# Six input projections of a fused transformer kernel started on x times its gain, ahead of the RMS norm

## The chip, the cores and the metric

The kernel runs on one core of a Trainium2 chip. TensorE (PE) multiplies, VectorE (DVE) and ScalarE (ACT) work on elements, GpSimd (POOL) does a few of them too, and SyncE (SP) issues the DMA transfers. Each engine takes the instructions of its own queue in order and waits on semaphores for the others. The metric is the time of the program on the device in microseconds, lower is better; the median of several runs counts.

## The reference, cut to what matters

Two transformer blocks over 512 tokens of width 1024 follow one another in fp32. The change touches the first steps only: the RMS norm of x with its gain, and the product with `w_in`.

```python
def rms_norm(x, g):
    y = xf * lax.rsqrt(jnp.mean(xf * xf, axis=-1, keepdims=True) + RMS_EPS)
    return y * g

h = rms_norm(x, norm_mix)
p = h @ w_in
p_rw = p_rw + (token_shift(p_rw) - p_rw) * mu_shift
r, k, v, wd, ad, gd, cb, cc, cx, ga, gb = jnp.split(p, offsets, axis=-1)
out_a = rwkv7_branch(r, k, v, wd, ad, gd, ...)
```

The branch makes a decay and a gate out of `wd` and `ad` by small (LoRA) products, a second gate out of `gd`, and a recurrence over the tokens out of r, k and v. Since 1/rms is one number per token, (x * gain / rms) @ w_in is the same as ((x * gain) @ w_in) / rms.

## The kernel before

Everything lies with the features on the 128 partitions and the 512 tokens along the free axis: x is 8 columns of 128x512, `w_in` is cut into blocks of 128 output features. Fp32 products go through three matmuls: each operand is split into a rounded high part (a cast, by ACT) and a low part (a subtraction, by DVE), and `mm_fm` adds high by high (line 182), high by low (183) and low by high (184) into one PSUM bank of 128x512. A block is 8 steps of three matmuls, 24 in all. `wload` brings half a block of weights per transfer (`wraw`, five buffers) and `wsplit` splits it into `whi` (four buffers) and `wlo` (three); the first two blocks, loaded with `early=True`, are split with POOL in place of DVE, into `we`.

The start runs like this. Four transfers bring x in pairs of columns. For each column ACT squares it (203, 206) and DVE and POOL in turn add the squares (207, 208). `sums` forms the sum over the partitions with small matmuls (146), `rsqrt` makes 1/rms by three Newton steps on DVE (134 to 139, tiles `rq_v`, `rq_t`, `rq_y`), `bcast` spreads it over all partitions by matmuls with the identity (192). Then, for each of the 8 columns, DVE forms `hx` = x * gain / rms (212), reading 1/rms from PSUM, and `split` makes `h` from it (152 and 153). Only then can a block of `w_in` be multiplied.

Blocks are used in this order: block 0 (`sa`: wd and ad), 1 and 2 (`sg`, `gsp`: gd), then, in four rounds of `prep`, k, r and v: blocks 3, 4, 5 in round 0, blocks 6, 7, 8 in round 1 and so on. `shift` mixes a block with its neighbour token: ACT scales it into `q` (236), DVE adds (237). `sa` goes through a tanh and a split to `wa`, which the LoRA products of each round need (`lora_mm`, 274). In a round the norm of k is a small product (292, from the square `sq`), eleven short DVE steps, `rb`, and a broadcast (314); a scan `cs` over the tokens gives the decay; then come `kk`, `f`, `m`, three pieces of `KB`, `r`, `rkk` and `vs`, with POOL doing some products (`f`, two of `AR`) among them. `prep_tail` (340, 344) of a round, the small products of `rkk` and `vs`, is called in the next round behind that round's k.

The code is ordered by the framework's scheduler, which puts each engine's instructions into a fixed queue before the run; pools with few buffers add waits on the readers of the older tile. The three pools of PSUM banks are `mm` (three banks), `sc` (two) and `ch` (three; they are first used in the chunks of the recurrence, far later).

Of the kernel before, what the change touches and what calls it, by code (L numbers as in the profile page):

```python
# [26 lines left out]
PI_BELOW = 3.1415925  # L27

# [17 lines left out]
def fused_kernel(ctx, tc, a, out):  # L46
# [72 lines left out]
    for i in range(4):  # L119
        nc.sync.dma_start(x0[:, 2 * i:2 * i + 2], a["xT"][:, 2 * i:2 * i + 2])  # L120
        if i == 0:
            nc.sync.dma_start(vc, a["vecs"])
# [35 lines left out]
    def wsplit(raw, shape, early=False):  # L158
        if early:
            w = reg.tile([128, 2] + shape[1:], F32R, tag="G4", bufs=4, name=nm("we"))  # L160
            split(raw, w[:, 0], w[:, 1], eng=G)
            return w[:, 0], w[:, 1]
# [78 lines left out]
    shift(proj_in(0, True), 12, sa)  # L241
# [955 lines left out]
```

## Time and profile before

| | us |
|---|---|
| median of 3 runs | 1345.91 |
| lowest, highest | 1342.25, 1346.05 |
| profiled execution, its own time | 1346.67 |
| its span in the profile | 1344.7 |

| engine | busy us | share of the span |
|---|---|---|
| PE (matmul) | 1303.4 | 97% |
| PE (weight load) | 1073.8 | 80% |
| DVE | 821.7 | 61% |
| ACT | 524.0 | 39% |
| POOL | 176.1 | 13% |

The times in the rows below are microseconds from the start of the span. A row of the timeline is one or several like instructions in a row: start, time they took together, engine, line, operation, output and inputs, and in brackets the idle time before it with what ended it. Neighbouring instructions of DVE and ACT overlap by some 0.05 us, so a pass shown with 0.69 us comes 0.62 us behind another. Matmuls overlap too: what counts is the distance of their starts.

### The profile page before, as it was taken

The numbers are of one execution on the slowest core, as the hardware profiler recorded it, in microseconds if no ns is written. First come the engines' busy times: TensorE is split into PE (matmuls) and PEld (weight loads), VectorE is DVE, ScalarE is ACT, GpSimd is POOL, SyncE is SP. The second block draws the span as 40 slices with busy tenths as digits, with TensorE's granted clock in tenths as the row PEclk, the third lists the DMA queues.
The fourth block names the chain that finished last, engine by engine and source line by source line (L and its number), as shares of the span: only waits on it lengthen the run. The fifth ranks groups of instructions, "written<-read, shape, count | busy, mean of one in ns | idle before, by whom it ended". The sixth has DMA issues, their size and how long they took to land.

```text
span 1344.7 us, 18356 instructions
## 1 busy us (share of the span) xinstructions
PE 1303.4 (97%) x6640; PEld 1073.8 (80%) x6640; DVE 821.7 (61%) x1640; ACT 524.0 (39%) x948; POOL 176.1 (13%) x185
## 2 busy tenths in 40 slices
PE   3999999999999999999999999999999999999997
PEld 2777888888879888878888888888878777788886
DVE  5677574848466755656844636544777566663455
ACT  4444332322335444454423423324344465333332
POOL 5113002010120020002021020120322000100003
PEclk9999998989999999999999999999999999999999
DMA  4222341323315522153644635323234223233331
GB/s 143 87 84 68 102 116 44 92 67 108 101 50 150 194 94 86 56 159 111 192 134 126 191 98 164 110 87 96 95 124 133 71 63 118 94 95 101 95 118 63
DMA packets 85211, 143.95 MB, mean 107 GB/s; under 512 B 21473, under 2 KB 21601, under 8 KB 85121
## 3 DMA queue, kind: packets, MB, share of 16 engines
q1 hardware_dynamic: 85120, 142.78, 34.2%
q8 instruction: 52, 0.85, 0.3%
q14 instruction: 39, 0.31, 0.1%
HBM read 136.19 MB, written 5.24 MB: 105 GB/s over the span
## 4 chain that ended last, share of the span: by engine, by line
PE 94%; DVE 3%; POOL 1%; DMA 1%; issue 0%; ACT 0%; SPq 0%; DVEq 0%; ACTq 0%; POOLq 0%
PE mm L182 26%; PE mm L183 25%; PE mm L184 25%; PE mm L628 1%; PE mm L627 1%; PE mm L629 1%; PE ch L986 1%; PE sc L386 1%; PE ch L948 1%; PE ch L467 1%; PE ch L458 1%; DMA x<-in_xT 1%; PE ch L462 1%; PE ch L491 1%; PE ch L443 0%
## 5 line engine op out<-in xcount | busy, mean ns | idle before, releaser
L152 ACT CAST whi<-wraw 128x512 fp32r<-128x512 f32 x406 | 251.6, 622 | 540.5 <-PE mm L183 468.8
L153 DVE TENSOR_TENSOR wlo<-wraw,whi 128x512 fp32r<-128x512 f32 x406 | 299.4, 739 | 222.3 <-PE mm L184 116.0
L182 PE MATMUL mm<-h,whi 128*128 128x512 f32 x328 | 131.6, 401 | 1.0 <-DVE k L237 1.0
L183 PE MATMUL mm<-h,whi 128*128 128x512 f32 x328 | 130.6, 398 | 0.0
L184 PE MATMUL mm<-h,wlo 128*128 128x512 f32 x328 | 130.1, 397 | 0.0
L182 PE MATMUL mm<-x2g,whi 128*128 128x512 f32 x256 | 100.2, 392 | 0.0
L184 PE MATMUL mm<-x2g,wlo 128*128 128x512 f32 x256 | 99.7, 390 | 0.0
L183 PE MATMUL mm<-x2g,whi 128*128 128x512 f32 x256 | 99.6, 389 | 0.0
L182 PE MATMUL mm<-ff,whi 128*128 128x512 f32 x256 | 99.6, 389 | 0.0
L183 PE MATMUL mm<-ff,whi 128*128 128x512 f32 x256 | 99.6, 389 | 0.0
L184 PE MATMUL mm<-ff,wlo 128*128 128x512 f32 x256 | 99.6, 389 | 0.0
L182 PEld LDWEIGHTS mm<-h,whi 128*128 128x128 f32 x328 | 62.3, 190 | 16.0 <-DVE k L237 2.6
L184 PEld LDWEIGHTS mm<-h,wlo 128*128 128x128 f32 x328 | 62.0, 189 | 13.1 <-issue 0.5
L183 PEld LDWEIGHTS mm<-h,whi 128*128 128x128 f32 x328 | 62.1, 189 | 12.7 <-issue 0.4
L852 POOL TENSOR_TENSOR X<-X,d 128x512 f32<-128x512 f32 x24 | 39.3, 1636 | 220.8 <-DVE d L850 220.8
L658 POOL TENSOR_TENSOR gt<-gt,nsq 128x512 f32<-128x512 f32 x21 | 27.7, 1321 | 291.4 <-ACT nsq L657 284.0
L182 PE MATMUL mm<-h2a,whi 128*128 128x512 f32 x152 | 60.7, 402 | 0.1
L183 PE MATMUL mm<-h2a,whi 128*128 128x512 f32 x152 | 60.3, 397 | 0.0
L184 PE MATMUL mm<-h2a,wlo 128*128 128x512 f32 x152 | 60.2, 396 | 0.0
L182 PE MATMUL mm<-h2b,whi 128*128 128x512 f32 x152 | 60.0, 394 | 0.0
L184 PE MATMUL mm<-h2b,wlo 128*128 128x512 f32 x152 | 59.5, 393 | 0.0
L183 PE MATMUL mm<-h2b,whi 128*128 128x512 f32 x152 | 59.4, 392 | 0.0
(467 smaller groups left out, 2724.1 us busy)
## 6 DMA issues: line engine op xcount, KB each, us to landing
wraw<-in_w_in SPq DMA_DIRECT2D x162, 256.0 KB, 2.6
wraw<-in_w_up SPq DMA_DIRECT2D x64, 256.0 KB, 2.6
wraw<-in_w_down SPq DMA_DIRECT2D x64, 256.0 KB, 2.8
adaraw<-in_w_ada SPq DMA_DIRECT2D x24, 512.0 KB, 3.7
wraw<-in_w_proj_b SPq DMA_DIRECT2D x16, 256.0 KB, 2.7
wraw<-in_w_k SPq DMA_DIRECT2D x16, 256.0 KB, 2.7
wraw<-in_w_proj_a SPq DMA_DIRECT2D x16, 256.0 KB, 2.7
wraw<-in_w_v SPq DMA_DIRECT2D x16, 256.0 KB, 2.7
```

The lines of the kernel that those rows point to most:

```text
L152: S.copy(hi, src)
L153: eng.tensor_tensor(lo, src, hi.bitcast(F32), op=ALU.subtract)
L182: PE.matmul(acc, lhsT=wh, rhs=xh, start=start and k == 0, stop=False)
L183: PE.matmul(acc, lhsT=wh, rhs=xl, start=False, stop=False)
L184: PE.matmul(acc, lhsT=wl, rhs=xh, start=False, stop=stop and k == n - 1)
L386: PE.matmul(pq[hd % 2][:, j * 128:(j + 1) * 128], lhsT=KB[p0:p0 + 64, j, n * 128:(n + 1) * 128], rhs=AR[p0:p0 + 64, j, n].rearrange("p q c ...
L458: PE.matmul(pu[ub:ub + 32, hs], lhsT=ZT[ub:ub + 32, c, hd, :], rhs=gsb[ub:ub + 32, hs], start=True, stop=True)
L462: PE.matmul(pg[ub + 32:ub + 64, hd * 64:(hd + 1) * 64], lhsT=gr[ub:ub + 32, hd, 32:64], rhs=VU[ub:ub + 32, tb, c, hd, :], start=False, sto ...
L467: PE.matmul(pu[ub + 32:ub + 64, hs], lhsT=ZT[ub + 32:ub + 64, c, hd, :], rhs=gsb[ub + 32:ub + 64, hs], start=True, stop=True)
L491: PE.matmul(py[kb:kb + 64, hd * 64:(hd + 1) * 64], lhsT=gr[:, hd, 64:128], rhs=VU[:, tb, c, hd, :], start=n == 0 and hd == 0, stop=hd == 7)
L658: G.tensor_tensor(self.acc, self.acc, sq, op=ALU.add)
L852: G.tensor_tensor(X[:, j], X[:, j], d, op=ALU.add)
```

## The change

Six transfers bring x now, one or two columns each, and between them go the first halves of the weights of blocks 0 to 5 (`first_weights`), with their second halves behind. As each column of x lands, `split` forms the high and low part of x * gain (`xg`, no 1/rms in it). The twelve halves of weights are split by ACT and DVE into `wf` and `we`. `first_mm(j)` multiplies column j with all six blocks; their six sums stand in six PSUM banks, three of `mm` and three of `ch`. The squares are added by DVE alone. The sums over the partitions are put behind the matmuls of column 5, the broadcast of 1/rms behind those of column 6. ACT copies 1/rms from PSUM to `rxs`; six DVE passes scale the six banks by it into `pf` (line 251 of the new code), and `proj_in` hands these out for blocks 0 to 5. `h` is formed behind that as before, from `rxs`, for the blocks from 6 on. The split with POOL is gone.

```diff
+    nc.sync.dma_start(x0[:, 0], a["xT"][:, 0])
+    nc.sync.dma_start(vc, a["vecs"])
+    first_weights(0, 0)
+    first_weights(1, 0)
+    nc.sync.dma_start(x0[:, 1], a["xT"][:, 1])
+    for i, j in ((2, 2), (3, 3), (4, 4), (5, 6)):
+        first_weights(i, 0)
+        nc.sync.dma_start(x0[:, j:min(j + 2, DB) if j > 3 else j + 1],
+                          a["xT"][:, j:min(j + 2, DB) if j > 3 else j + 1])
+    for i in range(NFIRST):
+        first_weights(i, 1)
...
+    first = [mmbank() for _ in range(3)] + [chbank() for _ in range(3)]
...
+    def first_mm(j):
+        for blk in range(NFIRST):
+            w = wf_[blk, j // 4]
+            cs_ = slice((j % 4) * 128, (j % 4 + 1) * 128)
+            mm_fm(first[blk], [(w[:, 0, cs_], w[:, 1, cs_])], [xg[j]], start=j == 0, stop=j == DB - 1)
+
     for j in range(DB):
-        acc = accx[j % 2]
-        if j < 2:
-            S.activation(acc, x0[:, j], AF.Square)
+        split(x0[:, j], xg[j][0], xg[j][1], scale=vcol("norm_mix", j))
+        if j % 4 == 0:
+            first_split(j // 4)
+        if j == 0:
+            S.activation(accx, x0[:, j], AF.Square)
         else:
             sq = tt("sqx")
             S.activation(sq, x0[:, j], AF.Square)
-            (V, G)[j % 2].tensor_tensor(acc, acc, sq, op=ALU.add)
-    V.tensor_tensor(accx[0], accx[0], accx[1], op=ALU.add)
-    rxb = bcast(rsqrt(sums(accx[0]), TB, 1.0 / D, 1e-6))
+            V.tensor_tensor(accx, accx, sq, op=ALU.add)
+        if j < DB - 2:
+            first_mm(j)
+    ssx = sums(accx)
+    first_mm(DB - 2)
+    rxb = bcast(rsqrt(ssx, TB, 1.0 / D, 1e-6))
+    first_mm(DB - 1)
+    rxs = tt("rxs")
+    S.copy(rxs, rxb)
+    pf = []
+    for blk in range(NFIRST):
+        f = tt("pf")
+        V.tensor_tensor(f, first[blk], rxs, op=ALU.mult)
+        pf.append(f)
...
     for j in range(DB):
         hf = tt("hx")
-        V.scalar_tensor_tensor(hf, x0[:, j], vcol("norm_mix", j), rxb, op0=ALU.mult, op1=ALU.mult)
+        V.scalar_tensor_tensor(hf, x0[:, j], vcol("norm_mix", j), rxs, op0=ALU.mult, op1=ALU.mult)
         split(hf, h[j][0], h[j][1])
...
-    def proj_in(blk, early=False):
+    def proj_in(blk):
+        if blk < NFIRST:
+            return pf[blk]
         p = mmbank()
-        mm_fm(p, wload(a["w_in"][blk], 0, DB, early), h)
+        mm_fm(p, wload(a["w_in"][blk], 0, DB), h)
         return p
...
-    shift(proj_in(0, True), 12, sa)
+    shift(proj_in(0), 12, sa)
```

How the queues change is seen from the instructions in their order. On DVE before, from the last step of 1/rms to the tile `k` of block 3 (names: output, then inputs; `wlo` rows are weights of coming blocks):

```order
L139 SCALAR_TENSOR_TENSOR rq_y_143<-rq_t_144,rq_y_143 128x4 [waits DVE_49]
L212 SCALAR_TENSOR_TENSOR hx_161<-x_106,vc,sc_156 128x512 [waits DMAHW0_49,PE_49]
...
L153 TENSOR_TENSOR h_2_112<-hx_161,h_2_112 128x512 [waits Activation_49]
...
L153 TENSOR_TENSOR h_3_113<-hx_189,h_3_113 128x512 [waits Activation_49]
...
L237 SCALAR_TENSOR_TENSOR sa_205<-mm_206,omu,q_241 128x512 [waits Activation_49,Pool_49]
L237 SCALAR_TENSOR_TENSOR sg_256<-mm_257,omu,q_292 128x512 [waits Activation_49,Pool_49]
L153 TENSOR_TENSOR wa<-sa_205,wa 128x512 [waits DVE_49,Activation_49]
...
L237 SCALAR_TENSOR_TENSOR k_351<-mm_352,omu,q_389 128x512 [waits Activation_49,Pool_49]
```

and on DVE now:

```order
L251 TENSOR_TENSOR pf_385<-mm_140,rxs_383 128x512 [waits PE_49,Activation_49]
...
L251 TENSOR_TENSOR pf_395<-ch_145,rxs_383 128x512 [waits PE_49]
L259 SCALAR_TENSOR_TENSOR hx_399<-x_106,vc,rxs_383 128x512
...
L259 SCALAR_TENSOR_TENSOR hx_427<-x_106,vc,rxs_383 128x512 [waits DVE_49]
L286 SCALAR_TENSOR_TENSOR sa_443<-pf_385,omu,q_444 128x512 [waits DVE_49,Activation_49,Pool_49]
L168 TENSOR_TENSOR h_49_398<-hx_423,h_49_398 128x512 [waits Activation_49]
L168 TENSOR_TENSOR h_49_398<-hx_427,h_49_398 128x512 [waits Activation_49]
L286 SCALAR_TENSOR_TENSOR sg_459<-pf_387,omu,q_460 128x512 [waits Activation_49,Pool_49]
L168 TENSOR_TENSOR wa<-sa_443,wa 128x512 [waits Activation_49]
L168 TENSOR_TENSOR lhl<-lraw_453,lhl 128x512 [waits DMAHW4_49,DMAHW2_49,Activation_49]
L286 SCALAR_TENSOR_TENSOR k_482<-pf_391,omu,q_483 128x512 [waits Pool_49]
```

The passes for `h` stood at the head of this stretch with 1/rms in front of them and no scaling; now the six scalings, each waiting for a bank, are in front of them, and `sa`, `wa` and `k` still behind.

On PE before, around the LoRA product of round 0 (274, here also of round 1), the norm of k (292, 314) and the tail of round 0 (340, 344); the rows left out between are block 4, 5 and 6:

```order
L184 MATMUL mm_352<-h_3_113,wlo_362 128x512
L274 MATMUL mm_416<-wa,lhl 128x512 [waits Activation_49]
...
L182 MATMUL mm_454<-h_2_112,whi_457 128x512 [waits DVE_49]
L292 MATMUL sc_395<-hsel,sq_393 128x2 [waits PE_49,Activation_49]
...
L314 MATMUL sc_437<-ident,rb_414 128x128 [waits DVE_49,PE_49]
...
L340 MATMUL sc_582<-hsel,rkk_496 128x2 [waits DVE_49,PE_49]
L344 MATMUL sc_588<-ident,vs_498 128x128 [waits DVE_49,PE_49]
L274 MATMUL mm_618<-wa,lhl 128x512
L182 MATMUL mm_656<-h_2_112,whi_659 128x512 [waits DVE_49]
```

and on PE now, from the last matmul of the six blocks to block 7 (`mm_676`); the rows left out after `mm_561` are the rest of block 6:

```order
L195 MATMUL ch_145<-xg_15_139,we_266 128x512
L323 MATMUL mm_510<-wa,lhl 128x512 [waits DVE_49,Activation_49]
...
L193 MATMUL mm_561<-h_48_397,whi_564 128x512
L341 MATMUL sc_489<-hsel,sq_487 128x2 [waits PE_49,Activation_49,Pool_49]
...
L363 MATMUL sc_531<-ident,rb_508 128x128 [waits DVE_49,PE_49]
...
L323 MATMUL mm_638<-wa,lhl 128x512 [waits Activation_49]
...
L389 MATMUL sc_602<-hsel,rkk_553 128x2 [waits DVE_49,PE_49]
L393 MATMUL sc_608<-ident,vs_555 128x128 [waits DVE_49,PE_49]
L193 MATMUL mm_676<-h_48_397,whi_679 128x512 [waits DVE_49]
```

Of the 72 matmuls of blocks 4, 5 and 6 that stood between the LoRA product of round 0 and the tail of that round, only the 24 of block 6 are left there. From block 7 on both queues hold the same instructions.

## Rows read from the trace of the kernel before

**Rows 1.** The page, part 1: busy us, share of the span, instructions.

```profile
PE 1303.4 (97%) x6640; PEld 1073.8 (80%) x6640; DVE 821.7 (61%) x1640; ACT 524.0 (39%) x948; POOL 176.1 (13%) x185
```

**Rows 2.** Table of stretches: length, then busy us of PE to POOL, clock, DMA, GB/s.

```profile
0.00:5.00 5.00, 0.00 (x0) 0.00 (x0) 0.00 (x0) 1.40 (x2) 2.99 (x22) 1.00 0.57 170
5.00:10.00 5.00, 0.00 (x0) 0.00 (x0) 1.47 (x9) 2.68 (x5) 0.43 (x1) 1.00 0.99 338
10.00:15.00 5.00, 0.00 (x0) 0.00 (x0) 3.15 (x3) 3.04 (x6) 4.92 (x6) 1.00 0.92 235
...
73.02:91.74 18.72, 18.71 (x88) 15.19 (x89) 14.00 (x28) 7.63 (x13) 4.82 (x8) 1.00 0.22 70
...
215.70:222.50 6.80, 6.80 (x32) 5.21 (x30) 1.38 (x2) 1.19 (x2) 1.25 (x4) 0.50 0.00 0
```

**Rows 3.** The waits of PE: us in total, times, longest.

```profile
PE sc L146 <- DVE accx L208: 16.5, 1, 16.5
```

**Rows 4.** The timeline of the first microseconds: start, us, what.

```profile
25.32 1.22 PE L182 MATMUL mm<-h,we 128*128 128x512 f32 x2 [1.49 <-ACT h L152]
...
30.18 0.63 PE L183 MATMUL mm<-h,we 128*128 128x512 f32 x1
...
30.61 0.63 PE L184 MATMUL mm<-h,we 128*128 128x512 f32 x1
...
37.15 0.39 PE L184 MATMUL mm<-h,we 128*128 128x512 f32 x1
...
37.83 0.39 PE L184 MATMUL mm<-h,we 128*128 128x512 f32 x1
```

**Rows 5.** The timeline of DVE while `h` is formed.

```profile
23.87 2.06 DVE L212 SCALAR_TENSOR_TENSOR hx<-x,vc,sc 128x512 f32<-128x512 f32 x3 [2.23 <-PE sc L192]
...
33.36 1.28 DVE L153 TENSOR_TENSOR h<-hx,h 128x512 fp32r<-128x512 f32 x2
```

**Rows 6.** The timeline of ACT at the start.

```profile
4.88 1.15 ACT L203 ACTIVATE accx<-x 128x512 f32<-128x512 f32 x2 [2.80 <-DMA x<-in_xT]
```

**Rows 7.** The timeline of DVE from block 0 to round 1.

```profile
39.12 0.75 DVE L237 SCALAR_TENSOR_TENSOR sa<-mm,omu,q 128x512 f32<-128x512 f32 x1 [3.27 <-ACT q L236]
...
41.57 0.69 DVE L153 TENSOR_TENSOR wa<-sa,wa 128x512 fp32r<-128x512 f32 x1 [0.35 <-ACT wa L152]
...
51.36 0.75 DVE L237 SCALAR_TENSOR_TENSOR k<-mm,omu,q 128x512 f32<-128x512 f32 x1 [0.34 <-ACT q L236]
...
56.88 0.42 DVE L295 TENSOR_SCALAR rb<-rq_y 128x512 f32<-128x512 f32 x1
...
57.67 1.23 DVE L302 TENSOR_TENSOR_SCAN cs<-state,tw 128x512 f32<-128x512 f32 x1
...
60.69 0.55 DVE L319 TENSOR_SCALAR f<-ta,ka,ka 128x512 f32<-128x512 f32 x1 [1.16 <-ACT ta L311]
...
61.75 1.78 DVE L153 TENSOR_TENSOR wlo<-wraw,whi 128x512 fp32r<-128x512 f32 x1
...
66.99 1.68 DVE L332 SCALAR_TENSOR_TENSOR rkk<-r,vc,f 128x512 f32<-128x512 f32 x1
...
69.20 0.74 DVE L237 SCALAR_TENSOR_TENSOR vs<-mm,omu,q 128x512 f32<-128x512 f32 x1
...
72.01 0.75 DVE L237 SCALAR_TENSOR_TENSOR k<-mm,omu,q 128x512 f32<-128x512 f32 x1 [0.17 <-ACT q L236]
```

**Rows 8.** The timeline of PE: the small products of round 0, block 7's start.

```profile
53.20 0.95 PE L292 MATMUL sc<-hsel,sq 128*128 128x2 f32 x8
...
57.45 1.13 PE L314 MATMUL sc<-ident,rb 128*128 128x128 f32 x8
...
72.95 0.50 PE L182 MATMUL mm<-h,whi 128*128 128x512 f32 x1
```

**Rows 9.** The timeline of POOL in round 0.

```profile
61.38 1.60 POOL L320 TENSOR_TENSOR f<-k,f 128x512 f32<-128x512 f32 x1 [1.49 <-DVE f L319]
```

More of the change, by code (lines that the diff above doesn't have):

```diff
@@ L27 @@
 PI_BELOW = 3.1415925
+NFIRST = 6
 def _two_pi_parts():
@@ L118, in fused_kernel, with first_weights @@
     x0 = reg.tile([128, DB, T], F32, tag="R", bufs=7, name="x0")
[L119 to L122, printed above, removed]
+    raw0 = {}
+    def first_weights(blk, half):
+        w = wp.tile([128, 4, 128], F32, tag="wraw", bufs=5, name=nm("wraw"))
+        nc.sync.dma_start(w, a["w_in"][blk][:, 4 * half:4 * half + 4, :])
+        raw0[blk, half] = w
+    nc.sync.dma_start(x0[:, 0], a["xT"][:, 0])
[9 more added lines that the diff above has]
+        first_weights(i, 1)
     def vcol(name, i=0, n=1):
@@ L156, in split, with wsplit @@
             V.scalar_tensor_tensor(lo, src, scale, hi.bitcast(F32), op0=ALU.mult, op1=ALU.subtract)
[L158 to L162, printed above, removed]
+    def wsplit(raw, shape):
         hi = wp.tile(shape, F32R, tag="whi", bufs=4, name=nm("whi"))
@@ L166, in wsplit, with wload @@
         return hi, lo
-    def wload(tiles, k0, nk, early=False):
+    def wload(tiles, k0, nk):
         ncol = tiles.shape[2]
@@ L174, in wload @@
             nc.sync.dma_start(raw, tiles[:, k:k + step, :])
-            hi, lo = wsplit(raw, [128, step, ncol], early)
+            hi, lo = wsplit(raw, [128, step, ncol])
             parts += [(hi[:, i, :], lo[:, i, :]) for i in range(step)]
@@ L194, in bcast, with first_split @@
         return p
-    hreg = [regionr("h0"), regionr("h1")]
-    h = pairs(hreg, DB)
-    accx = [tt("accx"), tt("accx")]
-    for j in range(DB):
-        acc = accx[j % 2]
-        if j < 2:
-            S.activation(acc, x0[:, j], AF.Square)
+    xgr = [regionr("xg0"), regionr("xg1")]
+    xg = pairs(xgr, DB)
+    first = [mmbank() for _ in range(3)] + [chbank() for _ in range(3)]
+    accx = tt("accx")
+    wf_ = {}
+    def first_split(half):
+        w4 = regionr("wf")
+        for blk in range(NFIRST):
+            if blk < 4:
+                w = w4[:, blk]
+            else:
+                w = reg.tile([128, 2, T], F32R, tag="G4", bufs=4, name=nm("we"))
+            split(raw0[blk, half].rearrange("p k c -> p (k c)"), w[:, 0], w[:, 1])
+            wf_[blk, half] = w
+    def first_mm(j):
[3 more added lines that the diff above has]
+            mm_fm(first[blk], [(w[:, 0, cs_], w[:, 1, cs_])], [xg[j]], start=j == 0, stop=j == DB - 1)
+    for j in range(DB):
+        split(x0[:, j], xg[j][0], xg[j][1], scale=vcol("norm_mix", j))
[3 more added lines that the diff above has]
+            S.activation(accx, x0[:, j], AF.Square)
         else:
@@ L206, in fused_kernel @@
             S.activation(sq, x0[:, j], AF.Square)
-            (V, G)[j % 2].tensor_tensor(acc, acc, sq, op=ALU.add)
-    V.tensor_tensor(accx[0], accx[0], accx[1], op=ALU.add)
-    rxb = bcast(rsqrt(sums(accx[0]), TB, 1.0 / D, 1e-6))
+            V.tensor_tensor(accx, accx, sq, op=ALU.add)
[8 more added lines that the diff above has]
+    pf = []
+    for blk in range(NFIRST):
+        f = tt("pf")
+        V.tensor_tensor(f, first[blk], rxs, op=ALU.mult)
+        pf.append(f)
+    hreg = [regionr("h0"), regionr("h1")]
+    h = pairs(hreg, DB)
     for j in range(DB):
         hf = tt("hx")
-        V.scalar_tensor_tensor(hf, x0[:, j], vcol("norm_mix", j), rxb, op0=ALU.mult, op1=ALU.mult)
+        V.scalar_tensor_tensor(hf, x0[:, j], vcol("norm_mix", j), rxs, op0=ALU.mult, op1=ALU.mult)
         split(hf, h[j][0], h[j][1])
@@ L254, in fused_kernel @@
         sg = tt("sg")
-        shift(proj_in(1 + i, i == 0), 13 + i, sg)
+        shift(proj_in(1 + i), 13 + i, sg)
         S.activation(sg, sg, AF.Tanh, scale=0.5)
```

## The prediction

> **What bounds the kernel now.** I read the shares of busy time first. PE is busy for 97% of the span [rows 1], so outside its start TensorE sets the time. A change pays only where PE waits. The table of stretches comes next: from 73.02 to 91.74 us PE is busy for 18.71 of 18.72 us [rows 2]. One round of `prep` is therefore full of matmuls, and any delay carried into that stretch is carried to the end. Third is the list of waits: the longest wait of PE, 16.5 us, is the first one, for the sum of squares of x [rows 3]. Its matmuls with `h` begin at 25.32 us, run 0.43 us apart at first (30.18 and 30.61) and later at three per 0.68 us (37.15 and 37.83), which is 0.227 us each [rows 4]. 512 columns at 0.43 us is the level of 1.2 GHz, at 0.227 us that of 2.4; the column of the granted clock reads 1.00 for both here, so I go by the pace.
>
> The place where I compare the two kernels is the first matmul of block 7. By then both have done blocks 0 to 6, the two small LoRA products of round 0 and 1, and the small products of round 0, and from there both PE queues hold the same work. It starts at 72.95 us before [rows 8].
>
> **Part 1, the early blocks (a gain).** The queue of SP now brings, up to the first half of block 5's weights, six columns of x, the vectors and six halves of weights: 12 x 0.262 + 0.07 = 3.2 MB. The first 5 us move 0.85 MB (170 GB/s), the next 5 us 1.69 MB (338 GB/s); the rest takes 2 to 3 us at 338 to 235 GB/s [rows 2], so that half is there at 12 to 13 us. The fourteen 128x512 passes of DVE up to its low part and ACT's casts run beside this: 0.64 us a pass on DVE (1.28 us for two [rows 5]) and 0.575 us on ACT (1.15 us for two [rows 6]), so the fourteen, from about 4.7 us on and with 1 us of waits for data, end near 14.8 us. PE works behind them from about 5.4 us on and has, held by block 5's low part, 30 of its 144 early matmuls behind it at about 15.1 us. The other 114 x 0.227 = 25.9 us, the sums (0.95 us, as the product of 8 parts at 53.20 [rows 8]) and the broadcast (1.13 us, as that at 57.45 [rows 8]) end at **43.1 us**. DVE and ACT have the early work behind them by 25 us, and the Newton steps of 1/rms lie beside the 18 matmuls of x's seventh column, so they cost nothing; without that cover they would cost PE some 2.5 us. If the slow pace held until 16 us, some 15 matmuls more would cost 0.2 us each: +3 us.
>
> **Part 2, the handover (a loss).** Now the order. Behind the early matmuls PE's queue has the LoRA product of round 0, which needs `wa`; behind that block 6, which needs `h`; then the norm of k, which needs `k`. On DVE the six scalings `pf` come first, then all sixteen passes for `h` (eight `hx`, eight low parts), and `sa`, `wa` and `k` of block 3 are behind those. Before the change the passes for `h` ran while PE was already at work on its first columns.
> - `pf`: each follows its bank; the last starts when the last bank is done, 43.1 + 0.2, and takes 0.75 us as other passes that read PSUM (`sa`, `k` [rows 7]): 44.0 us.
> - fourteen passes for `h` ahead of `sa`: 14 x 0.64 = 9.0 us. Three `hx` took 2.06 us from PSUM [rows 5]; from SBUF I take the 0.64 us of the low parts; by 0.69 us for `hx` it would be 0.4 us more. `sa` ends at 53.7 us.
> - `sa`'s end to `wa`'s end was 39.87 to 42.26, 2.4 us [rows 7]: 56.1 us. So PE stands still from 43.1 to about 56 us.
> - five more passes to `k` (3.3 us) and about 1.6 us of waits for five passes of ACT between them: `k` ends at **61.0 us**. Before it ended at 52.11 us [rows 7]: 8.9 us later.
>
> **Part 3, the chain from k to v (a smaller gain).** The norm's small product began 1.1 us after `k` [rows 7, 8]. Now PE has six LoRA matmuls (three pairs, 1.3 us) and 13 of block 6 ahead of it: at the slow pace 5.6 us, to 63.0 us; at the fast one 3.0 us, and then `k` decides, 61.9 us. I take 62.6 us, 9.4 us behind the 53.20 us of before [rows 8]. What follows to the scan and `f` has the same passes as before, so the scan starts at 57.67 + 9.4 = 67.1 us and `f` at 60.69 + 9.4 = 70.1 us [rows 7]. From `f`'s start to `vs`'s end DVE took 9.25 us, with three splits of weights in between, which are not there any more. Against this stands POOL: beside its product `f` of 1.60 us [rows 9] a DVE pass with two operands in SBUF took 1.78 us in place of 0.64 [rows 7], and `rkk`, beside the next product of POOL, 1.68 us [rows 7]. In the new order `KB<-f,ip` waits for POOL's `f` and meets POOL's next product. So: `f` 0.55, POOL 1.75, `KB` 2.2, two more `KB` 0.95, `r` 0.66, `rkk` 1.68, `vs` 0.7: 8.5 us. `vs` ends at 78.6 us. Without the meeting it would be 1.6 us less.
>
> The Trainium skill, SBUF — State Buffer, section "Who interferes with whom", says that a VectorE instruction with two SBUF inputs and a GpSimd instruction that reads SBUF keep each other out until the first is done. The passes of 1.78 and 1.68 us agree. By that rule the 8.5 us hold; without it the sum below would be 1.6 us smaller.
>
> PE has run out of work by then: its LoRA product of round 1 is done near 72 us, and the products of `rkk` and `vs` wait. Block 7 needs the bank that `k` of round 1 reads, one pass after `vs`: **79.4 us**, against 72.95: 6.5 us late.
>
> **Part 4, the clock.** Two stretches of PE without work, of 13 and of 6 to 7 us, are new. After the first wait of before, 14 matmuls ran at 0.43 us until 31.4 us, at a cost of 14 x 0.2 = 2.8 us. In mid-kernel the granted clock was 0.50 for 6.80 us [rows 2] while PE had small matmuls only, so it does fall again. The slow stretch behind the first gap is covered by the chain of part 3; behind the second it is PE's own. I take 2.5 us, between nothing and 2.8.
>
> **What else changes.** POOL loses three additions and four splits; DVE gets one addition, four splits and the eight low parts of x*norm_mix, all in the first 25 us; of the first 15 it was busy for 4.6 [rows 2]. The other transfers of SP come in the same order as before. Later blocks 6 and up meet the same buffers. I cost all these at nothing.
>
> **Sum.** 6.5 + 2.5 = +9.0 us on the profiled execution, 1346.7 us, gives 1355.7; that execution lies 0.8 us above the median of the runs, 1345.9 us. So **1355 us**.
>
> **Rivals.**
> - *DVE never waits (no change).* From the first `pf` at 39.9 us (one bank of 18 matmuls after the broadcast's end, 39.0) to `vs` the passes of DVE sum to six `pf` at 0.7, sixteen for `h` at 0.64, eleven Newton steps at 0.2, the scan with 1.15 and 21 others at 0.6 in the mean: 4.2 + 10.2 + 2.2 + 1.15 + 12.6 = 30.3 us. If nothing held them up, `vs` would end at 70.2 and block 7 start at 71.0 us, 1.9 us early, with no clock to lose: 1344 us. For it: DVE was dense from 60.69 to 69.94 us. Against it: the alternation with ACT from `sa` to `k` had waits before too. Chance 0.16.
> - *The early lead is kept (faster).* If PE ran on from 43.1 us through block 6 and the small products without a wait, 1 + 5.4 + 2.1 + 2.5 = 11 us, block 7 would start at 54 us, 19 us early: 1327 us. It decides at where the sixteen passes for `h` stand: behind `k`, not ahead of it, they would make `k` end at 51 us. The order on DVE speaks against it; even then the chain from `k` to `vs` takes 18 us. Chance 0.07.
> - *The start is slower too.* If the data of part 1 come at the 235 GB/s of 10 to 15 us [rows 2] throughout, 3.2 MB take 13.6 us from 1.8 us on, and 30 matmuls are done some 3 us later; the same price holds if the slow pace lasts until 16 us. Then 1358 us. For it: x now comes in smaller pieces. Against it: weights in the same pieces ran at 338 GB/s with x. Chance 0.15.
>
> The Trainium skill, DMA: Bandwidth & Descriptors, section "Measured", tells to batch transfers to 1 MiB or more for three quarters of the peak, which speaks against cutting x from 512 KB to 256 KB pieces. By that rule this last rival would be the likely one, and the sum 3 us larger; the trace, with 338 GB/s from pieces of 256 and 512 KB in flight together, does not bear it out.
>
> **How the numbers follow.** The forecast has 0.62. Its unknowns: the clock (-2.5 to +0.3), POOL's meeting (-1.6), the start (up to +3), the norm's product (-0.7 to +0.4). That is 1349 to 1359. The range must take in the rival without change and the slow start: 1344 to 1361, which leaves out the fast case and a little above. A measurement of this kernel tells about 0.3% (4 us) from no change. Faster by more than that: 0.07. Within it: the first rival and the low end of the forecast, 0.16. Slower: 0.77.
>
> **What the new profile would show.** Early matmuls from 5 to 6 us on, ending at 43 us; a wait of PE of about 13 us ahead of the LoRA product, put down to DVE or ACT (`wa`); sixteen passes for `h` on DVE between the last `pf` and `wa`; `k` of round 0 at 60 to 61 us; a second wait of 6 us ahead of the product of `rkk`; block 7 at 79 us at the slow pace. If PE's first wait is below 5 us, or block 7 starts before 73 us, I am wrong. If block 7 starts late but the end does not move, a later stretch had slack that I do not see.

## The result and the profile after the change

| | before | after |
|---|---|---|
| median, us | 1344.31 (4 runs) | 1357.28 (4 runs) |
| lowest, highest | 1342.25, 1346.05 | 1355.38, 1361.50 |
| profiled execution | 1346.67 | 1355.38 |
| its span | 1344.7 | 1353.7 |

The changed kernel takes 1.0089 times as long as the kernel before, with a 95% interval of 1.0066 to 1.0113. Beside other kernels in a later group on one chip it took 1.0061 times as long (1.0038 to 1.0085). So it is slower, by some 7 to 13 us (the differences of the medians in the two groups). The forecast was 1355 us.

The busy shares, the line that answers [rows 1], hardly moved. The same work is done, and TensorE is busy for a point less of the span:

```profile
PE 1306.1 (96%) x6640; PEld 1074.0 (79%) x6640; DVE 829.8 (61%) x1661; ACT 529.0 (39%) x957; POOL 166.3 (12%) x178
```

The list of PE's waits answers [rows 3] (us in total, times, longest). The 16.5 us for the squares of x are gone. Three waits stand in their place, for the LoRA products of rounds 0 and 1 and for `rkk`:

```profile
PE mm L323 <- ACT lhl L167: 12.9, 1, 12.9
PE sc L389 <- DVE rkk L381: 7.9, 2, 5.6
...
PE mm L323 <- ACT ta L360: 2.3, 1, 2.3
```

The table of stretches, with the columns of [rows 2], shows where the new idle time lies, and that the granted clock is at 0.50 (1.2 GHz) in and behind both gaps:

```profile
5.00:10.00 5.00, 3.25 (x7) 1.94 (x8) 2.94 (x6) 2.76 (x5) 0.00 (x0) 1.00 0.96 308
10.00:15.00 5.00, 4.99 (x14) 3.41 (x13) 4.98 (x9) 5.00 (x10) 0.00 (x0) 1.00 1.04 406
...
26.50:38.00 11.50, 11.50 (x56) 9.65 (x55) 1.47 (x9) 0.00 (x0) 0.00 (x0) 1.00 0.33 109
...
45.00:50.00 5.00, 0.47 (x3) 0.05 (x1) 5.00 (x9) 1.85 (x3) 0.00 (x0) 0.84 0.00 0
50.00:55.00 5.00, 0.00 (x0) 0.00 (x0) 5.00 (x8) 3.04 (x5) 0.10 (x1) 0.50 0.00 0
55.00:60.00 5.00, 1.65 (x6) 0.86 (x6) 4.48 (x8) 4.69 (x10) 3.34 (x4) 0.50 0.00 0
...
75.00:80.00 5.00, 0.58 (x3) 0.61 (x4) 4.82 (x6) 1.30 (x2) 1.84 (x4) 0.50 0.00 0
80.00:85.00 5.00, 5.00 (x17) 4.05 (x18) 0.83 (x2) 1.88 (x3) 0.11 (x1) 0.50 0.01 3
```

From 26.5 to 38 us PE is busy throughout, DVE for 1.47 of 11.5 us and ACT for none. From 50 to 55 us it is the other way round: PE does nothing and DVE is busy for all 5 us. PE's timeline, which answers [rows 4] and [rows 8], gives the steps: the broadcast of 1/rms, the last early matmul, the LoRA product behind the first gap, the norm product of round 0, the products of `rkk` and `vs` behind the second gap, and the first matmul of block 7.

```profile
40.30 1.05 PE L203 MATMUL sc<-ident,rq_y 128*128 128x128 f32 x8
...
45.08 0.39 PE L195 MATMUL ch<-xg,we 128*128 128x512 f32 x1
...
58.35 1.82 PE L323 MATMUL mm<-wa,lhl 64*128 64x512 f32 x6 [12.88 <-ACT lhl L167]
64.05 0.97 PE L341 MATMUL sc<-hsel,sq 128*128 128x2 f32 x8
...
79.42 1.84 PE L389 MATMUL sc<-hsel,rkk 128*128 128x2 f32 x8 [5.56 <-DVE rkk L381]
81.12 1.09 PE L393 MATMUL sc<-ident,vs 128*128 128x128 f32 x4
82.18 0.79 PE L193 MATMUL mm<-h,whi 128*128 128x512 f32 x1
```

Block 7 starts at 82.18 us, before the change at 72.95 [rows 8]: 9.2 us late. DVE's timeline, which answers [rows 5] and [rows 7], shows the line that PE waits for: six `pf`, then `hx` and the low parts of `h` in turn, and `sa` only behind fourteen of the sixteen; then `k`, and 17 us later `vs`. The first row is the last addition of squares: 1/rms could be formed from 24.2 us on, and `pf` starts at 42.16.

```profile
23.52 0.69 DVE L239 TENSOR_TENSOR accx<-accx,sqx 128x512 f32<-128x512 f32 x1
...
42.16 2.00 DVE L251 TENSOR_TENSOR pf<-mm,rxs 128x512 f32<-128x512 f32 x3 [3.77 <-PE mm L195]
...
46.12 2.06 DVE L259 SCALAR_TENSOR_TENSOR hx<-x,vc,rxs 128x512 f32<-128x512 f32 x3
...
55.24 0.75 DVE L286 SCALAR_TENSOR_TENSOR sa<-pf,omu,q 128x512 f32<-128x512 f32 x1
...
62.40 0.74 DVE L286 SCALAR_TENSOR_TENSOR k<-pf,omu,q 128x512 f32<-128x512 f32 x1
...
79.20 0.74 DVE L286 SCALAR_TENSOR_TENSOR vs<-pf,omu,q 128x512 f32<-128x512 f32 x1
```

### The profile page after: what moved, and what is told of

It is laid out like the page before. It is cut to its first block, busy times and chain, and to the rows that moved or that the text cites. A ratio compares the mean times of both kernels' runs of the same rounds, so it can differ in the third digit from the quotient of the medians.

```text
span 1353.7 us, 18371 instructions
## 1 busy us (share of the span) xinstructions
PE 1306.1 (96%) x6640; PEld 1074.0 (79%) x6640; DVE 829.8 (61%) x1661; ACT 529.0 (39%) x957; POOL 166.3 (12%) x178
## 4 chain that ended last, share of the span: by engine, by line
PE 93%; DVE 5%; POOL 1%; issue 1%; ACT 0%; DMA 0%; SPq 0%; DVEq 0%; ACTq 0%; POOLq 0%
PE mm L193 25%; PE mm L194 25%; PE mm L195 25%; PE mm L677 1%; PE mm L676 1%; PE mm L678 1%; PE ch L1035 1%; PE sc L435 1%; PE ch L997 1%; PE ch L507 1%; PE ch L516 1%; PE ch L511 1%; PE ch L540 1%; PE ch L492 0%; PE sc L1028 0%
## 5 line engine op out<-in xcount | busy, mean ns | idle before, releaser
L167 ACT CAST whi<-wraw 128x512 fp32r<-128x512 f32 x398 | 246.6, 622 | 527.9 <-PE mm L194 461.5
L168 DVE TENSOR_TENSOR wlo<-wraw,whi 128x512 fp32r<-128x512 f32 x398 | 289.5, 729 | 219.1 <-PE mm L195 114.6
L193 PE MATMUL mm<-h,whi 128*128 128x512 f32 x296 | 119.6, 404 | 0.0
L194 PE MATMUL mm<-h,whi 128*128 128x512 f32 x296 | 118.6, 401 | 0.0
L195 PE MATMUL mm<-h,wlo 128*128 128x512 f32 x296 | 117.9, 398 | 0.0
L193 PEld LDWEIGHTS mm<-h,whi 128*128 128x128 f32 x296 | 56.5, 191 | 13.7 <-DVE k L286 1.1
L195 PEld LDWEIGHTS mm<-h,wlo 128*128 128x128 f32 x296 | 56.3, 190 | 12.1 <-issue 0.5
L194 PEld LDWEIGHTS mm<-h,whi 128*128 128x128 f32 x296 | 56.5, 191 | 11.8 <-issue 0.4
```

The source lines that it names most:

```text
L167: S.copy(hi, src)
L168: eng.tensor_tensor(lo, src, hi.bitcast(F32), op=ALU.subtract)
L193: PE.matmul(acc, lhsT=wh, rhs=xh, start=start and k == 0, stop=False)
L194: PE.matmul(acc, lhsT=wh, rhs=xl, start=False, stop=False)
L195: PE.matmul(acc, lhsT=wl, rhs=xh, start=False, stop=stop and k == n - 1)
```

## The experiments

The kernels ran in three groups, each beside the kernel before on one chip, and the expectations number them so: first the passes for `h` behind `k`, the fillers, three early blocks, and the first kernel with an early chain; then the yardstick, 1/rms with `h` in front, the second kernel with an early chain, and block 6 ahead; last, 1/rms alone and the third kernel with an early chain. They stand here by subject.

The theory behind the forecast is that the handover costs: what DVE has in line between the early matmuls and `vs` of round 0. It left open which part of that line matters. Rivals were the slower start, the order on PE, and the clock. The times are ratios to the kernel before, measured in the same group with a 95% interval. The marks in the traces are the end of `k` of round 0 and the start of block 7. Before the change they are 52.1 and 72.95 us, after it 63.1 and 82.18 us. The changed kernel ran a second time as a yardstick:

> The changed kernel itself, unaltered, beside the others of this group on one chip, so that they can be compared with it. Expected 1.007 to 1.011 times the kernel before, block 7 at 82 us, k of round 0 at 63 us, 1/rms broadcast at 40.3 us, all as in its first profile.

Measured: 1356.1 us, 1.0061 (1.0038 to 1.0085), and block 7 at 83.16 us. Up to block 7 the trace came out as before within 1 us; the lower end of the expected ratio was missed by a little, and the two measurements overlap. Behind block 7 the two profiles differ by more: the product of `rkk` of round 1 starts at 105.53 us, against 102.41 in the first profile. The runs below are compared with the first profile, so steps of 1 us in a mark prove little.

**The passes for `h` behind `k`.**

```diff
-    for j in range(DB):
-        hf = tt("hx")
...
+    def form_h():
+        for j in range(DB):
+            hf = tt("hx")
...
         shift(proj_in(3 + 3 * j), 4 + j, k)
+        if j == 0:
+            form_h()
```

> The changed kernel with the sixteen passes for h moved behind k of round 0 on DVE (the regions are handed out in another order so that this is possible). Theory (handover): between the broadcast of 1/rms and v of round 0 DVE has some 30 us of passes in line, and the place of the sixteen inside that line decides only which of its results come late. So wa comes near 49 us (58.0), the LoRA product of round 0 near 50 us and k of round 0 at 53 to 55 us (63.1), but the scan stays at 67 to 69 us and block 7 starts at 80 to 82 us (82.2): 1355 to 1358 us. Rival (place): the passes cost because they stand ahead of k, as the prediction's fast case has it; then everything behind k is 9 us earlier, block 7 starts near 73 us and the time is 1346 to 1349 us. Rival (start): nothing moves but k, and the time stays at 1357 us; told apart from the first by the scan only if that moves.

Measured: 1353.3 us, 1.0044 (1.0030 to 1.0059). DVE's timeline:

```profile
51.55 0.75 DVE L288 SCALAR_TENSOR_TENSOR k<-pf,omu,q 128x512 f32<-128x512 f32 x1
...
66.75 1.23 DVE L355 TENSOR_TENSOR_SCAN cs<-state,tw 128x512 f32<-128x512 f32 x1
```

`k` comes 10.8 us earlier, the scan only 2.1 us (68.82 us in the changed kernel) and block 7 2.4 us (79.76). The time lies 1.7 us below the range of the theory and well above that of the rival. The profiled execution, with 1358.9 us, was the longest of the five, so the marks and the median are not of the same execution. The passes cost in either place. The rival by which they cost because they stand ahead of `k` falls, and with it the condition that the prediction gave its fast case.

**1/rms earlier, alone, and with `h` in front.** The first kernel moves only the small products on PE:

```diff
-        if j < DB - 2:
+        if j < 4:
             first_mm(j)
     ssx = sums(accx)
-    first_mm(DB - 2)
+    first_mm(4)
     rxb = bcast(rsqrt(ssx, TB, 1.0 / D, 1e-6))
-    first_mm(DB - 1)
+    for j in (5, 6, 7):
+        first_mm(j)
```

> One half of the second group's second run: in the changed kernel the sum of squares and the broadcast of 1/rms are moved forward on PE behind the fourth and fifth columns of x, and nothing else. Theory (DVE's line): 1/rms is broadcast near 33 us in place of 40, but DVE's queue has the six scalings first, and they wait for their banks, which are done when the early matmuls end (45 us); the passes for h stay behind them, so k of round 0 stays at 62 to 63 us, block 7 at 81 to 83 us and the time at that of the changed kernel, 1.006 to 1.010 times the kernel before. Rival (the late 1/rms alone costs): k of round 0 and block 7 come 6 to 8 us earlier, 1.001 to 1.003 times the kernel before.

Measured: 1358.1 us, 1.0094 (1.0071 to 1.0117): no gain. `k` of round 0 ends at 62.4 us and block 7 starts at 82.3 us, as in the changed kernel. The broadcast starts at 31.41 us, nearly 9 us earlier, and DVE waits out the gain, because `pf` stands first in its queue and needs a finished bank:

```profile
41.45 1.98 DVE L252 TENSOR_TENSOR pf<-mm,rxs 128x512 f32<-128x512 f32 x3 [11.94 <-PE mm L195]
```

The second kernel has the same edit, and the loop that makes `pf` stands behind the one that makes `h` (the regions are handed out in the other order, as in the kernel with `h` behind `k`):

```diff
     for j in range(DB):
         hf = tt("hx")
...
+    pf = []
+    for blk in range(NFIRST):
+        f = tt("pf")
+        V.tensor_tensor(f, first[blk], rxs, op=ALU.mult)
```

> The changed kernel with the sum of squares and the broadcast of 1/rms moved forward on PE, from behind the seventh column of x to behind the fourth and the fifth, and the passes for h put ahead of the six scalings on DVE. All work is the same. Theory (late 1/rms): the changed kernel loses because 1/rms, ready to be formed at 25 us, is broadcast at 40 us behind 126 early matmuls, so that DVE's line from h to v of round 0 begins that much later. Here 1/rms is there near 33 us, the sixteen passes for h lie beside the early matmuls (34 to 45 us), k of round 0 comes at 52 to 53 us (63), v of round 0 ends at 69 to 70 us (79.9) and block 7 starts at 71 to 73 us (82.2; 72.95 before the change): about 10 us less than the changed kernel, 1345 to 1348 us, level with the kernel before. PE still waits some 9 us for the chain. Rival (start or clock): the early part and the slow pace are unchanged, so the time stays within 3 us of the changed kernel. Rival (order on PE): LoRA ahead of block 6 holds PE back; then some 4 us are gained, not 10.

Measured: 1350.1 us, 1.0016 (1.0001 to 1.0031), 6.0 us less than the changed kernel in the same group, where the changed kernel lost 7.0. DVE and PE:

```profile
33.80 2.08 DVE L254 SCALAR_TENSOR_TENSOR hx<-x,vc,rxs 128x512 f32<-128x512 f32 x3 [3.62 <-ACT rxs L249]
...
53.38 0.75 DVE L287 SCALAR_TENSOR_TENSOR k<-pf,omu,q 128x512 f32<-128x512 f32 x1
```

```profile
70.24 1.84 PE L390 MATMUL sc<-hsel,rkk 128*128 128x2 f32 x8 [6.25 <-DVE rkk L382]
...
73.00 0.79 PE L195 MATMUL mm<-h,whi 128*128 128x512 f32 x1
```

Block 7 starts 9.2 us earlier, where it stood before the change. So sixteen passes of DVE behind the early matmuls in place of beside them are the 9 us by which block 7 came late. The earlier 1/rms alone gained nothing; the passes ahead of `pf` without it were not run. The time came down by less than the expected 10 us. Both gaps of PE are still there (5.2 and 6.2 us), and block 7 begins at the slow pace; since block 7 is back at its old place all the same, neither the slower start nor the slow pace can be the main cause of the loss.

**Block 6 ahead of the LoRA product on PE.** Its bank is taken and its 24 matmuls are written ahead of `sa`:

```diff
+    p6 = [mmbank()]
+    mm_fm(p6[0], wload(a["w_in"][6], 0, DB), h)
+
     sa = tt("sa")
```

> The changed kernel with block 6 ahead of the LoRA product of round 0 on PE. Theory (late 1/rms; DVE's line bounds): block 6 runs from 48 to 58 us as h comes in, PE's longest wait shrinks to some 3 us, yet k of round 0 stays at 63 us, the scan comes at most 1 us earlier and block 7 starts at 81 to 82 us: 1355 to 1358 us. Rival (order on PE): the 5.4 us of block 6 are what the queue lost; block 7 starts near 77 us and the time is 1350 to 1352 us.

Measured: 1358.5 us, 1.0073 (1.0043 to 1.0104).

```profile
46.88 0.50 PE L193 MATMUL mm<-h,whi 128*128 128x512 f32 x1 [2.09 <-ACT h L167]
...
59.95 1.65 PE L328 MATMUL mm<-wa,lhl 64*128 64x512 f32 x6 [2.56 <-ACT lhl L167]
...
83.79 0.79 PE L193 MATMUL mm<-h,whi 128*128 128x512 f32 x1
```

The wait of 12.9 us is gone, and block 7 starts no earlier: PE's idle time only moved. It came even 1.6 us later than in the changed kernel's first profile and 0.6 us later than in the yardstick's, where the expectation had 0 to 1 us earlier. The place of block 6 on PE is no cause here.

**Matmuls that nothing reads in both gaps.** The kernel adds 68 matmuls whose result is not used:

```diff
+    def filler(n):
+        w = wf_[5, 1]
+        for i in range(n):
+            tc.keep_in_program_order(PE.matmul(fillb, lhsT=w[:, 0, 0:128], rhs=w[:, 1], start=True, stop=True))
+
+    filler(fills[0])
```

> The changed kernel with matmuls that nothing reads: 48 of 512 columns behind the early blocks, where PE stands still for 13 us, and 20 behind the LoRA product of round 1, where it stands still again. They keep PE at work, and so show what the slow clock costs. Theory (handover, with the clock as a term of 2.5 us): the order of all other work stays, the LoRA product of round 0 takes 1.4 us in place of 1.8, the small products behind the second gap and the first matmuls of block 7 run at the fast pace, block 7 starts at 80 to 81.5 us: 1353 to 1355.5 us, 2 to 4 us less than the changed kernel. Rival (clock): the slow pace is most of the loss, block 7 starts near 75 us: 1346 to 1349 us. If the gaps are no cause of the slow pace, the granted clock stays at 0.50 there and the time at 1357 us or above.

Measured: 1358.5 us, 1.0092 (1.0063 to 1.0122). The expected 2 to 4 us less did not come. The table of stretches and PE's timeline:

```profile
45.00:57.00 12.00, 10.91 (x49) 8.69 (x47) 11.69 (x20) 7.05 (x12) 0.94 (x4) 1.00 0.00 0
65.00:70.00 5.00, 2.13 (x13) 1.72 (x13) 3.83 (x15) 1.21 (x2) 0.00 (x0) 0.74 0.19 62
70.00:75.00 5.00, 5.00 (x14) 3.12 (x14) 2.49 (x4) 2.34 (x4) 1.88 (x4) 0.50 0.01 2
```

```profile
69.15 2.04 PE L375 MATMUL sc<-ident,rb 128*128 128x128 f32 x8 [2.87 <-DVE rb L356]
71.12 3.29 PE L333 MATMUL mm<-wa,lhl 64*128 64x512 f32 x6
```

In the first gap the clock stays at 1.00. Then it falls all the same, behind a wait of 2.9 us in which no filler stands, and the LoRA product of round 1 takes 3.29 us for six matmuls. Block 7 starts at 82.57 us, 0.4 us later than in the changed kernel, but at the fast pace, and the product of `rkk` of round 1 starts at 101.44 us against 102.41. From block 7's start to that product it is 18.9 us here, 18.8 us before the change, 20.2 us in the changed kernel's first profile and 22.4 us in the yardstick's, where the matmuls run 0.43 us apart until 91.9 us:

```profile
91.43 0.61 PE L193 MATMUL mm<-h,whi 128*128 128x512 f32 x1
```

So the slow pace behind block 7 is worth about 1.4 us in one profile of the changed kernel and 3.5 us in the other. The clock is not the main cause of the loss: block 7 starts as late without the slow pace in the first gap. In the times none of this can be seen.

**Three early blocks.**

```diff
-NFIRST = 6
+NFIRST = 3
...
-    first = [mmbank() for _ in range(3)] + [chbank() for _ in range(3)]
+    first = [chbank() for _ in range(NFIRST)]
```

> The changed kernel with three early blocks in place of six: blocks 0 to 2 are multiplied with x*norm_mix as x lands, blocks 3 to 5 with h as before the change. Theory (handover): PE then has three blocks (16 us) to do while DVE goes from h through k to v of round 0. The 72 early matmuls end near 24 us, h follows by 39 us with block 3 behind it, blocks 4, 5 and 6 cover the chain, and block 7 starts at 62 to 66 us (72.95 before the change, 82.2 after it): 1335 to 1339 us, faster than both. Rival (start): the transfers in smaller pieces and the splits at the start are what costs; they are nearly the same here, so the time is 1350 us or more. Rival (clock at the gap): the new wait between the early blocks and h costs the fast pace again; 1340 to 1345 us.

Measured: 1347.3 us, 1.0002 (0.9985 to 1.0018): the loss is gone, and the expected gain did not come. DVE's and PE's timeline and a stretch:

```profile
47.24 0.74 DVE L287 SCALAR_TENSOR_TENSOR k<-mm,omu,q 128x512 f32<-128x512 f32 x1
...
68.20 0.74 DVE L287 SCALAR_TENSOR_TENSOR vs<-mm,omu,q 128x512 f32<-128x512 f32 x1
...
72.00 0.75 DVE L287 SCALAR_TENSOR_TENSOR k<-mm,omu,q 128x512 f32<-128x512 f32 x1 [0.17 <-ACT q L286]
```

```profile
45.00:50.00 5.00, 1.96 (x6) 1.57 (x6) 1.63 (x3) 1.98 (x3) 0.00 (x0) 0.50 0.17 61
```

Block 7 starts at 72.94 us, where it started before the change (72.95), and not at 62 to 66 us. x still comes in the smaller pieces, though with half of the weights between them, and the loss is gone. That speaks against the rival "start"; the kernel with 1/rms earlier and `h` in front, whose start is unaltered, speaks against it more strongly. I had `h` done by 39 us with PE running on. It was, at 39.8 us, but `wa` and `k` stood behind it as before, PE waited again and ran at the slow pace to 57 us. `vs` ended 1 us earlier than before the change (68.94 against 69.94) and `k` of round 1 at the same place (72.75 against 72.76).

**The chain started early.** Three kernels follow from what the runs above showed. In all of them `pin` keeps PE's instructions in the order in which they are written. In the first, the second half of x's columns is multiplied block by block, the small products stand between the blocks in the written order, each `pf` stands where its block is used, and `h` is made in pieces along the chain:

```diff
+    ssx = sums(accx)
+    pinned[0] = True
+    last_mm(0)
+    rxb = bcast(rsqrt(ssx, TB, 1.0 / D, 1e-6))
+    last_mm(3)
+    last_mm(1)
```

> Six early blocks as in the change, but the 1/rms is formed as soon as x is there and not behind the early matmuls: the second half of the columns is multiplied block by block (0, 3, 1, 2, 4, 5), the sum of squares goes ahead of it, the LoRA product and the norm of k between, each scaling by 1/rms stands where its block is needed, and the passes for h are spread over the chain. Theory (handover): 1/rms is broadcast near 31 us in place of 41, k of round 0 is there at 36 to 38 us, the early matmuls end near 49 us with the small products among them, and block 6 follows at once as h comes in. PE has no wait over 3 us from 6 us on, v of round 0 comes at 56 to 60 us, and block 8 starts 8 to 15 us earlier than before the change (which has it at 78.4 us): 1331 to 1338 us. Rival (DVE's work is the bound whatever the order): the chain and h together last until 65 to 70 us, block 7 starts no earlier than before: 1343 to 1347 us. Rival (start): 1350 us or more.

Measured: 1344.8 us, 0.9991 (0.9975 to 1.0008): level with the kernel before. `k` of round 0 is there at 38.5 us, and by 69.6 us PE has block 7 behind it. Then it gives all of that back:

```profile
74.22 1.87 PE L359 MATMUL sc<-hsel,sq 128*128 128x2 f32 x8 [4.48 <-ACT sq L356]
```

The norm product of round 1 stands ahead of block 8 in PE's queue and waits for a `k` that ends at 72.8 us, again the mark of the kernel before. `v` of round 0 ends at 66.3 us where 56 to 60 was expected, and block 8 starts at 80.60 us in place of 8 to 15 us earlier than before the change. (By the count of matmuls it starts at 80.85 us before the change; the 78.4 of the expectation is a misreading.) The next kernel put blocks 7, 8 and 9 ahead of the small products and made 1/rms still earlier:

```diff
+            early[6] = block(6)
+            pw, pa = lora_mm(1)
+            early[7] = block(7)
+            early[8] = block(8)
```

> The kernel of the fourth run, with what its profile showed mended: 1/rms is formed as soon as the squares are summed (sum of squares on PE behind the third column, low parts of the second half of the weights behind the squares on DVE, broadcast behind one block), blocks 6, 7, 8 and 9 stand on PE ahead of the small products that wait for DVE (there PE stood still from 69.6 to 80.6 us with block 8 ready), and the two gate inputs are shifted behind round 1. Theory (late 1/rms, and the order on PE after it): 1/rms is there near 28 us, k of round 0 at 33 to 35 us, v of round 0 at 58 to 62 us; PE waits for nothing over 3 us from 6 us on, and the small product of rkk of round 1 stands at 80 to 85 us (91.7 before the change, 102.4 after it): 1333 to 1340 us. Rival (DVE's work bounds two rounds whatever the order): that product stands at 88 us or later: 1343 to 1347 us.

Measured: 1351.0 us, 1.0018 (1.0002 to 1.0035), above the ranges of the theory and of the rival. The product of `rkk` of round 1 starts at 86.4 us, between the 80 to 85 of the theory and the 88 of the rival; that of round 2 starts at 115.5 us, 2.7 us later than before the change (112.8). `k` of rounds 0 and 1 end at 35.6 and 63.9 us, then:

```profile
84.57 1.64 PE L336 MATMUL mm<-wa,lhl 64*128 64x512 f32 x3 [5.17 <-DVE r L307]
...
93.14 0.80 PE L201 MATMUL mm<-h,whi 128*128 128x512 f32 x1 [3.93 <-DVE k L307]
```

PE has the blocks done and waits for banks that DVE must read first, and `k` of round 2 ends at 93.1 us (93.8 before the change). Here the lead of PE was worth nothing, because the chain from `k` to `k` did not lead as well. The third puts the small products between the columns of a block, gives the later blocks the `ch` banks, and shifts the gate inputs behind round 2:

```diff
+    def part(blk, c0=0, c1=DB):
+        if c0 == 0:
+            early[blk] = chbank()
+            wts[blk] = wload(a["w_in"][blk], 0, DB)
+        mm_fm(early[blk], wts[blk][c0:c1], h[c0:c1], start=c0 == 0, stop=c1 == DB)
...
+            part(5 + 3 * j, 6 if j == 1 else 3, 8)
+            if j < 3:
+                part(6 + 3 * j)
+                lora[j + 1] = lora_mm(j + 1)
+                part(7 + 3 * j, 0, 5)
```

> As the third run of the second group, where PE was 16 us ahead at 75 us and gave all of it back between 78 and 98 us, because the next round's k came late (92 us): a product of the chain stood behind a whole block on PE, blocks waited for banks that DVE frees, and the gate inputs stood ahead of k. Here the small products stand between the columns of a block, where the chain wants them, the later blocks use the three banks that the early ones leave free and the LoRA products the other three, and the gate inputs are shifted behind round 2. Theory (the chain of rounds from k to k sets the pace once PE is ahead, and its 27 to 29 us in that run were waits of order): k of rounds 0, 1, 2, 3 at 35, 62 to 64, 82 to 86 and 103 to 107 us (52, 73, 94, 115 before the change), PE dense again from there, 1.0 per cent less than the kernel before within 0.3: 1331 to 1340 us. Rival (a round of the chain takes 21 us or more beside the passes for the weights, whatever the order on PE): k of round 3 at 111 us or later, 0.4 per cent less than before at the most: 1341 us or more.

Measured: 1336.9 us, 0.9927 (0.9907 to 0.9947): faster than both kernels, and the expected 0.990 within 0.003. `k` of the four rounds, on DVE's timeline:

```profile
33.94 0.75 DVE L312 SCALAR_TENSOR_TENSOR k<-pf,omu,q 128x512 f32<-128x512 f32 x1
...
62.24 0.74 DVE L312 SCALAR_TENSOR_TENSOR k<-ch,omu,q 128x512 f32<-128x512 f32 x1
...
81.43 0.74 DVE L312 SCALAR_TENSOR_TENSOR k<-ch,omu,q 128x512 f32<-128x512 f32 x1
...
104.03 0.75 DVE L312 SCALAR_TENSOR_TENSOR k<-ch,omu,q 128x512 f32<-128x512 f32 x1 [0.46 <-ACT q L311]
```

They end at 34.7, 63.0, 82.2 and 104.8 us, where the kernel before has 52.1, 72.8, 93.8 and 114.9. The last is 10 us earlier, and the time 8.5 us less. PE is not quite dense behind it: it idles for 4.0 us between 100 and 130 us (1.2 us before the change). The changes of banks and of order in it were not run apart, so which of them gave the gain is not shown.

## Why the prediction was right, point by point

**The bound.** That a delay carried into the rounds is carried to the end held: 9.2 us at block 7, 9.0 us at the end of the span, though the two are not the same 9 us (see the sum).

**Part 1.** The first early matmul came at 5.57 us (5.4), but the early part ended at 45.3 us instead of 43.1. The weights of block 1 were late. ACT's cast of them waited 2.2 us for the transfer and ran at 7.75 us, with PE idle for 1.2 us behind it, and the slow pace held until about 14.2 us. By 15.1 us PE had started 20 early matmuls and not 30, and ten at 0.227 us are the 2.2 us.

```profile
7.75 0.62 ACT L167 CAST wf<-wraw 128x512 fp32r<-128x512 f32 x1 [2.22 <-DMA wraw<-in_w_in]
```

This is a part of the rival "the start is slower too", by its second condition and not by its first: the transfers ran at 308 and 406 GB/s, not at 235. The rule of the Trainium skill, DMA: Bandwidth & Descriptors, section "Measured", on small transfers is not borne out by these rates either (its figures are of transfers issued from GpSimd, and these were issued from SP). What cost was the wait for one half of the weights and the slow pace behind it.

**Part 2.** The order on DVE was read rightly, and so was the gap: 13 us were forecast, 12.9 came. `k` ended at 63.1 us instead of 61.0, late by the 2 us of part 1. The fast bound for the norm's product behind it should read 62.1 us by its own terms (61.0 + 1.1), not 61.9; the product started at 64.05.

**Part 3.** Block 7 was forecast at 79.4 us and came at 82.18. Of these 2.8 us, some 2 come from part 1. The stretch from `f` to `vs` took 7.75 us in place of 8.5: the first piece of `KB` met POOL's product and took 1.38 us (0.41 us for its like without it), `rkk` took 1.68 us beside the next one, and the rest ran free.

```profile
74.50 1.38 DVE L374 TENSOR_TENSOR KB<-f,ip 128x256 f32<-128x256 f32 x1 [1.16 <-POOL f L369]
...
76.41 0.41 DVE L375 TENSOR_TENSOR KB<-f,ip 128x256 f32<-128x256 f32 x1
...
77.59 1.68 DVE L381 SCALAR_TENSOR_TENSOR rkk<-r,vc,f 128x512 f32<-128x512 f32 x1
```

```profile
74.42 1.18 POOL L376 TENSOR_TENSOR AR<-kk,pp 128x512 f32<-128x512 f32 x1
```

That such a pass of DVE and such a product of POOL keep each other out is what the Trainium skill, SBUF — State Buffer, section "Who interferes with whom", says. The trace agrees: the first piece of `KB` ends at 75.88 us, just behind POOL's product at 75.60. The effect was smaller than I had put down. The miss is behind it: the products of `rkk` and `vs` took 1.84 and 1.09 us at the slow pace, where I had 0.8 us from `vs` to block 7 and not 2.2.

**Part 4.** The term of 2.5 us was put behind block 7's start. There the first seven matmuls ran 0.43 us apart, at a cost of 7 x 0.2 = 1.4 us, which agrees with the kernel with fillers. Another 1.4 us lay ahead of it, in the two small products of part 3. So the whole was 2.8 us, sized well and placed half wrong. The yardstick's profile, with 3.5 us behind block 7, shows that the next profile of the same kernel can differ by 2 us in this term. One ground given for the term, that the clock fell at 215.70 us while PE had small matmuls only, was read wrongly: seven of the 32 in that stretch have 128x512 outputs.

**The sum.** That makes 9.2 + 1.4 = 10.6 us behind block 7's first matmuls, not 9.0; the product of `rkk` of round 1 starts at 102.41 us, before the change at 91.74. The profiled span ended 9.0 us later because slow stretches of the clock fell elsewhere later on, which no step of the prediction spoke of. The changed kernel has one at 144 us that the kernel before has not. It lacks the one of [rows 2] at 215.70: the second row is the same work, 9 to 12 us later, and the clock is at 1.00 there.

```profile
144.00:147.40 3.40, 3.40 (x12) 2.71 (x11) 0.00 (x0) 1.67 (x3) 0.00 (x0) 0.51 0.11 43
227.70:231.70 4.00, 4.00 (x36) 3.11 (x34) 1.27 (x2) 1.20 (x2) 1.42 (x4) 1.00 0.00 0
```

With the matmuls of the two profiles matched by their order from block 7 on, the changed kernel is 10.8 us late at 85 us of its own time, 12.0 us at 147, 9.2 us at 232, 6.6 us at 286, 8.8 us at 300 and 9.1 us at the last one; nearly all of these steps lie at slow stretches of one kernel or the other. So the size was right to 1.5 us by steps, and closer by chance.

**What else changes.** DVE was said to get one addition of squares more; it gets three, seven in place of four. That is some 1.2 us more of DVE in the first 25 us, which the prediction put at nothing.

**The rivals.** "DVE never waits" had 30.3 us of passes from the first `pf` to `vs`; the trace has 37.8 us (42.16 to 79.94), with DVE waiting for PE, ACT and POOL in between. "The early lead is kept" named the right obstacle and the wrong condition: with the passes for `h` behind it `k` does end at 52.3 us (51 was said), yet block 7 starts at 79.8 us and not at 54. What decides is the whole chain of rounds. This is what the prediction lacked for its rivals: it took the place of 1/rms (40 us, though the squares are summed at 24.2 us) as given.

## What to carry to other kernels

Work that is made independent of a slow value is a gain only if the value itself does not come later for it: see where the new work stands in the queues relative to the chain that makes the value, and what DVE does while PE runs ahead. Here a chain across engines was about as long as PE's work per round, and starting PE earlier moved nothing by itself; the chain had to be started earlier too, with its small products between the large ones and enough banks for both. Before a gain is booked, follow the lead to the next place where two engines meet.

## What the runs showed of the hardware

In the first gap fillers held the clock up, and it fell at a wait where none stood. With them the granted clock was 1.00 from 45 to 57 us, 0.74 from 65 to 70 us with PE busy for 2.13 of 5 us, and then 0.50 from 70 to 75 us with PE busy for all of them. A busy PE does not bring the fast pace back at once: in the yardstick's profile block 7 starts at 83.16 us behind 2.8 us of work without a gap, and its matmuls stay 0.43 us apart until 91.9 us.

The slow stretches of the clock lie at other places in each profile, and the kernel before took 1342.82 to 1351.16 us in one group. In that group the five executions above 1349 us had a mean granted clock of 0.987 or 0.988, the fifteen others 0.989 to 0.993. So the spread goes with the clock; whether the clock is all of it was not tried. Steps of 1 to 2 us are better read in the trace, at marks like block 7's start, than from the times.
